# Attention values of branch A issued as unbroken trains of matmuls, ahead of other waiting matmuls

## The chip, the cores and the metric

The kernel runs on one core of a Trainium2 chip. The metric is the device time of one execution in microseconds (us). Each time in this document is from the runs of the kernel or from a hardware profile of one execution. The engines are named as in the profile: PE is TensorE's matmul, PEld its weight load, DVE is VectorE, ACT is ScalarE, POOL is GpSimd and SP is SyncE, which issues all transfers. L915 means line 915 of the kernel.

## The reference

One encoder layer is applied to two groups of requests (a prompt and a sample, 1024 tokens each, width 1024) with the same weights. The input is normalised and modulated, one combined projection gives everything that the two attention branches need, and the two results are gated, projected, merged and projected again:

```python
h = rms_norm(x, norm_g) * (1.0 + scale) + shift
proj = einsum('bsd,de->bse', h, w_in)
qa, ka, va, za, qb, kb, vb, zb, ga, gb = split(proj, ...)
# branch A: 8 query heads, 2 key/value heads, head width 64, two-dimensional rotary positions
oa = gqa_attention(rope(rms_norm(qa)), rope(rms_norm(ka)), va) * silu(za)
# branch B: 4 heads, the difference of two softmax maps, values 128 wide
ob = headnorm(diff_attention(qb, kb, vb, lam)) * silu(zb)
merged = sigmoid(ga) * (oa @ w_proj_a) + sigmoid(gb) * (ob @ w_proj_b)
y = x + gate * (merged @ w_out)
```

Branch A is plain attention: softmax over all 1024 keys, then probabilities times values:

```python
s = einsum('bqgrd,bkgd->bgrqk', q, k) / sqrt(64)
p = softmax(s)
o = einsum('bgrqk,bkgd->bqgrd', p, v)
```

Everything is in fp32.

## The kernel before, in words

The two groups are worked one after the other. For each, a start computes the normalised input (for group 0 from the beginning, for group 1 behind group 0's output projection), then come the projections, branch A's attention, branch B's attention, the gates, the merge and the output projection. Most matmuls take operands split into a high and a low part, in three products; the value matmuls of both branches take plain fp32.

Branch A's attention is cut into 32 units a group: a unit is two query heads that share a key/value head, for a tile of 128 queries. For each of its two heads `scores` runs four 512-wide matmuls (L846, L847) into one of two score banks, then DVE takes the maximum (L848), ACT scales it (L849) and takes the exponential (L850). `flip` transposes the 128x1024 probabilities in 32x32 blocks on DVE (L891) and issues four transfers from SP (L896) that put the blocks into the tile `pT` (the tiles named q in the profile), half of it for each head. The value step `a_values` (L908 on) then takes for each of eight chunks of 128 keys and each of the two heads one matmul: weights are the 128x64 values of the chunk, the moving side is 128x128 of the transposed probabilities, and the output is one half of the partitions of the bank `acc`. The loop runs over chunks, and within a chunk over the heads e = 0, 1, so that head 0 stands in the left 64 columns of the array and head 1 in the right 64. So there are 16 value matmuls a unit, 512 a group. ACT copies the bank out (L922), and every second unit a transfer stores it (L925). There is a single bank for this.

What sets the order is a scheduler. The Python code writes the attention as a generator and weaves it with other generators (projections of later heads, the z, g gates: L608, L819, L668) by weights: `ATT_W` scales how fast a phase's attention advances against its filling, `IN_A` gives the filling a head start. A phase is one piece of this: 0 and 1 are branch A's two halves, 2 and later are branch B's heads. The recorded instructions then go to a scheduler with a model of the machine, which sends each engine the instruction that it takes for the best next one among those that could run, by a priority that follows the order of recording. `tc.high_priority(offset=n)` moves what is recorded inside it n places ahead; all of the attention's steps stand in one of `AHEAD = 100`. Each engine then runs its instructions strictly in the order that the scheduler has set.

```python
            with tc.high_priority(offset=AHEAD):
                ...
                    next(vals[n], None)
```

Of the kernel before, what the change touches and what calls it, by code (L numbers as in the profile page):

```python
# [23 lines left out]
NCH = D // P  # L24
# [16 lines left out]
Z_HEAD = (7, 6)  # L41
Z_HEAD_A = (-0.3, -0.32)
ATT_W = (
    (0.825, 1.067, 1.07, 1.093, 1.03, 1.769),
    (0.938, 1.664, 1.177, 1.271, 0.764, 1.144),
)
IN_A = (
    (0.3, -0.07, 0.7, 0.05, 0.25, 0.15),
    (0.1, -0.05, 0.33, 0.3, -0.03, 0.55),
)  # L50
Z_A = (
# [21 lines left out]
AHEAD = 100  # L73
PV_LAG = 2
A_WAIT = 1
A_CUTS = ()

WHOLE = (True, True)

# [30 lines left out]
def kernel(ctx: ExitStack, tc: tile.TileContext, t: dict):  # L110
    nc = tc.nc
# [18 lines left out]
    def nm(s):  # L130
        uid[0] += 1
        return f"{s}_{uid[0]}"
# [40 lines left out]
    def mtile(tag, shape, dt=F32, bufs=None):  # L173
        return mpool.tile(shape, dt, tag=tag, name=nm(tag), bufs=bufs)
# [733 lines left out]
    def a_values(u):  # L908
        acc = ps_a.tile([P, 512], F32, tag="a", name=nm("a"))[:, :P]
        pT = u["pT"].bitcast(F32).rearrange("p (i t c b) -> p t c i b", i=4, t=2, c=8)  # L910
        for _ in range(A_WAIT):
            yield 1
        for k in range(NCH):
            for e in range(2):
                nc.tensor.matmul(acc[e * 64 : e * 64 + 64], u["v"](k), pT[:, e, k], start=(k == 0), stop=(k == 7))  # L915
            if k in A_CUTS:
                yield 1
        t = u["qt"] % 2
        if t == 0:
            turned["o"] = mtile("oo", [P, 256])  # L920
        o = turned["o"]
        nc.scalar.activation(o[:, t * P : (t + 1) * P], acc, AF.Copy)  # L922
        pr = u["pr"]
        if t:
            dma(u["od"][pr // 2][:, (pr % 2) * 256 : (pr % 2 + 1) * 256], o)  # L925
        yield 1
# [408 lines left out]
```

## Time and profile before

| | |
|---|---|
| median of 3 runs | 2003.58 us (2002.83 to 2007.69) |
| the profiled execution | 2004.5 us, its span 2002.7 us |
| granted TensorE clock, mean over the span | 0.993 |
| PE busy | 1951.8 us, 97% of the span |
| DVE, ACT, POOL busy | 61%, 43%, 20% of the span |
| value matmuls of branch A (L915) | busy 195.4 us, 2048 records, mean 281 ns of one |

The span is the time from the first to the last instruction; the device time is a little longer. "Busy" is the time in which at least one instruction of the row runs. Matmuls are pipelined: a 128x512 one lasts 0.39 us in the profile, but in a row they start 0.227 us apart, so steps are read from starts. An fp32 value matmul is two passes, and the profile has a record for each. The first value matmul of group 0 starts at 137.9 us and branch A of that group lasts until about 592; that of group 1 lasts from 1151 to 1484.

### The profile page before, as it was taken

The numbers are of one execution on the slowest core, as the hardware profiler recorded it, in microseconds if no ns is written. First come the engines' busy times: TensorE is split into PE (matmuls) and PEld (weight loads), VectorE is DVE, ScalarE is ACT, GpSimd is POOL, SyncE is SP. The second block draws the span as 40 slices with busy tenths as digits, with TensorE's granted clock in tenths as the row PEclk, the third lists the DMA queues.
The fourth block names the chain that finished last, engine by engine and source line by source line (L and its number), as shares of the span: only waits on it lengthen the run. The fifth ranks groups of instructions, "written<-read, shape, count | busy, mean of one in ns | idle before, by whom it ended". The sixth has DMA issues, their size and how long they took to land.

```text
span 2002.7 us, 32130 instructions
## 1 busy us (share of the span) xinstructions
PE 1951.8 (97%) x11430; PEld 1606.1 (80%) x11430; DVE 1213.9 (61%) x1824; ACT 853.1 (43%) x1839; POOL 400.7 (20%) x766
## 2 busy tenths in 40 slices
PE   6899999999999999999999999999999999999999
PEld 4778777777788888877889977788888899877787
DVE  4765565333457857786575665665536776877731
ACT  3544444233455645442423444554435554643210
POOL 0433200001232524100023312100044332400000
PEclk9999999999999999999999999999999999999999
DMA  9134566453435533788562274676633443478622
GB/s 320 39 90 134 132 187 167 127 136 102 111 109 160 143 104 81 209 260 277 194 198 71 86 186 127 174 190 163 165 98 97 124 110 99 126 222 281 213 100 74
DMA packets 277630, 299.55 MB, mean 150 GB/s; under 512 B 37664, under 2 KB 228320, under 8 KB 277472
## 3 DMA queue, kind: packets, MB, share of 16 engines
q1 hardware_dynamic: 277472, 297.51, 52.4%
q8 instruction: 92, 1.51, 0.3%
q14 instruction: 66, 0.54, 0.1%
HBM read 137.91 MB, written 42.04 MB: 90 GB/s over the span
## 4 chain that ended last, share of the span: by engine, by line
PE 84%; DMA 6%; DVE 5%; ACT 2%; issue 1%; POOL 1%; SPq 1%; DVEq 0%; ACTq 0%; POOLq 0%
PE f L819 24%; PE f L608 19%; PE a L915 9%; PE s L846 6%; PE f L1119 5%; PE s L847 5%; PE a L944 4%; PE s L1119 3%; PE f L1088 3%; PE s L1088 2%; PE s L106 1%; DMA row<-zd 1%; PE f L668 1%; DVE m L848 1%; DVE p L890 1%
## 5 line engine op out<-in xcount | busy, mean ns | idle before, releaser
L819 PE MATMUL f<-u,w 128*128 128x512 f32 x2184 | 577.2, 398 | 2.2 <-ACT ev L801 1.5
L608 PE MATMUL f<-w,u 128*128 128x256 f32 x3264 | 478.5, 288 | 4.2 <-DVE u L106 1.7
L819 PEld LDWEIGHTS f<-u,w 128*128 128x128 f32 x2184 | 397.5, 188 | 92.5 <-issue 14.7
L608 PEld LDWEIGHTS f<-w,u 128*128 128x128 f32 x3264 | 434.2, 191 | 37.4 <-issue 14.6
L848 DVE TENSOR_REDUCE m<-s 128x1 f32<-128x1024 f32 x256 | 310.7, 1218 | 227.3 <-PE s L847 225.3
L891 DVE STREAM_TRANSPOSE p<-p 128x1024 f32<-128x1024 f32 x192 | 238.4, 1242 | 94.6 <-ACT p L850 81.1
L847 PE MATMUL s<-u,sw 128*128 128x512 f32 x512 | 206.3, 404 | 0.0
L915 PE MATMUL a<-q,u 128*64 128x128 f32 x2048 | 195.4, 281 | 0.0
L915 PEld LDWEIGHTS a<-q,u 128*64 128x64 f32 x2048 | 129.8, 136 | 66.7 <-issue 49.4
L205 DVE TENSOR_TENSOR w<-st,w 128x512 fp32r<-128x512 f32 x188 | 125.4, 699 | 68.6 <-ACT w L204 66.7
L204 ACT ACTIVATE w<-st 128x512 fp32r<-128x512 f32 x188 | 108.7, 625 | 129.9 <-DMA st<-in_w_in_dram 52.7
L850 ACT ACTIVATE p<-s,m,rsB 128x1024 f32<-128x1024 f32 x128 | 154.2, 1205 | 5.2 <-DVE p L890 1.6
L850 ACT ACTIVATE p<-s,m,rsA 128x1024 f32<-128x1024 f32 x128 | 154.2, 1205 | 4.0 <-PE a L915 0.2
L1088 PE MATMUL f<-u,w 128*128 128x512 f32 x576 | 141.4, 395 | 5.1 <-ACT u L1060 3.0
L764 POOL TENSOR_TENSOR row<-row,gB 128x96 f32<-128x96 f32 x64 | 30.2, 472 | 549.0 <-ACT row L629 548.9
L1088 PEld LDWEIGHTS f<-u,w 128*128 128x128 f32 x576 | 108.2, 189 | 29.7 <-ACT u L1060 3.4
L944 PE MATMUL a<-q,u 128*128 128x256 f32 x512 | 126.0, 381 | 3.0 <-DMA q<-p 1.6
L671 DVE TENSOR_TENSOR u<-f,u 64x256 fp32r<-64x256 f32 (+1 forms) x208 | 84.1, 406 | 61.3 <-ACT u L670 55.8
L846 PE MATMUL s<-u 128*128 128x512 f32 x256 | 110.8, 433 | 4.2 <-ACT p L850 4.1
L847 PEld LDWEIGHTS s<-u,sw 128*128 128x128 f32 x512 | 97.0, 190 | 20.0 <-issue 5.0
L1119 PE MATMUL f<-u,w 128*128 128x512 f32 x480 | 111.2, 389 | 0.0
L628 ACT ACTIVATE row<-f 128x256 f32<-128x256 f32 (+1 forms) x104 | 38.5, 370 | 167.0 <-PE f L608 162.7
(191 smaller groups left out, 2216.9 us busy)
## 6 DMA issues: line engine op xcount, KB each, us to landing
q<-p SPq DMA_DIRECT2D x768, 128.0 KB, 2.8
st<-in_w_in_dram SPq DMA_DIRECT2D x128, 256.0 KB, 3.4
zd<-ev SPq DMA_DIRECT2D x96, 256.0 KB, 2.7
sw<-u SPq DMA_DIRECT2D x256, 64.0 KB, 2.1
p<-zd SPq DMA_DIRECT2D x64, 256.0 KB, 4.3
u<-in_w_ada_dram SPq DMA_DIRECT2D x16, 512.0 KB, 8.9
od<-oo SPq DMA_DIRECT2D x64, 128.0 KB, 2.5
st<-in_w_in_dram SPq DMA_DIRECT2D x64, 128.0 KB, 2.8
```

The costliest lines, as they stand in the source:

```text
L205: nc.vector.tensor_tensor(out=wl, in0=st, in1=wh.bitcast(F32), op=ALU.subtract)
L608: nc.tensor.matmul(ps, lt[c][:, sl], w[c][:, wi, :], start=(k == 0), stop=(k == 23))
L819: nc.tensor.matmul(ps, w[c][:, wi, e * P : (e + 1) * P], rt[c], start=(k == 0), stop=(k == 23),)
L846: nc.tensor.matmul(s[:, sl], q, k[:, sl], start=True, stop=False)
L847: nc.tensor.matmul(s[:, sl], sw, k[:, sl], start=False, stop=True)
L848: nc.vector.tensor_reduce(out=m, in_=s, axis=AX.X, op=ALU.max, negate=True)
L850: nc.scalar.activation(pt.rearrange("p (j c a) -> p j c a", j=4, c=8), s.rearrange("p (c a j) -> p j c a", c=8, j=4), AF.Exp, scale=rs, bi ...
L891: nc.vector.transpose(pt, pt)
L915: nc.tensor.matmul(acc[e * 64 : e * 64 + 64], u["v"](k), pT[:, e, k], start=(k == 0), stop=(k == 7))
L944: nc.tensor.matmul(acc, u["v"][:, k], pT[:, k], start=(k == 0), stop=(k == 7))
L1088: nc.tensor.matmul(ps, w[:, c, wi, d * P : (d + 1) * P], o[:, oi, :], start=(k == 0), stop=(k == 11))
L1119: nc.tensor.matmul(ps, w[c][:, wi, e * P : (e + 1) * P], m[:, mi, :], start=(k == 0), stop=(k == 23))
```

## The change

Three things. In `a_values` the 16 matmuls of a unit are recorded inside a second priority block, 200 places ahead (`TRAIN`), and the heads are taken in the order 1, 0. The possible pause between chunks (`A_CUTS`, empty before) is gone. Two numbers that weave the phases of group 0's branch B are others: the attention's weight in phase 3 and the filling's head start in phase 2.

```diff
 ATT_W = (
-    (0.825, 1.067, 1.07, 1.093, 1.03, 1.769),
+    (0.825, 1.067, 1.07, 1.192, 1.03, 1.769),
     (0.938, 1.664, 1.177, 1.271, 0.764, 1.144),
 )
 IN_A = (
-    (0.3, -0.07, 0.7, 0.05, 0.25, 0.15),
+    (0.3, -0.07, 0.65, 0.05, 0.25, 0.15),
     (0.1, -0.05, 0.33, 0.3, -0.03, 0.55),
 )
...
-A_CUTS = ()
+TRAIN = 200
...
         for _ in range(A_WAIT):
             yield 1
-        for k in range(NCH):
-            for e in range(2):
-                nc.tensor.matmul(acc[e * 64 : e * 64 + 64], u["v"](k), pT[:, e, k], start=(k == 0), stop=(k == 7))
-            if k in A_CUTS:
-                yield 1
+        with tc.high_priority(offset=TRAIN):
+            for k in range(NCH):
+                for e in (1, 0):
+                    nc.tensor.matmul(
+                        acc[e * 64 : e * 64 + 64], u["v"](k), pT[:, e, k], start=(k == 0), stop=(k == 7)
+                    )
```

What this does to the order on PE shows best in a unit from the middle of group 0's branch A (its accumulator is a_4202). Before, near the end of that unit; L819 and L608 are projections that fill:

```order
L608 MATMUL f_3978<-w_3955,u_433 128x256
L819 MATMUL f_4052<-u_632,w_3713 128x512
L915 MATMUL a_4202<-q_4027,u_728 64x128
L819 MATMUL f_4052<-u_631,w_3713 128x512
L915 MATMUL a_4202<-q_4027,u_728 64x128
L608 MATMUL f_3978<-w_3955,u_433 128x256
L608 MATMUL f_3978<-w_3955,u_434 128x256
```

The unit's 16 value matmuls stand one by one in 16 places. The same unit on PE after the change:

```order
L819 MATMUL f_4052<-u_649,w_3713 128x512
L819 MATMUL f_4052<-u_648,w_3713 128x512
L608 MATMUL f_4096<-w_3955,u_275 128x256
L916 MATMUL a_4202<-q_4027,u_728 64x128 x16
L608 MATMUL f_4096<-w_3955,u_275 128x256
L608 MATMUL f_4096<-w_3955,u_276 128x256
```

All 16 follow each other, at a place where one fill tile has just ended and the next has begun. Not every unit is whole: the last unit of each group's branch A is still cut, here that of group 0 on PE (accumulator a_5519; L668 are transposes of projected rows):

```order
L819 MATMUL f_5090<-u_433,w_5073 128x512
L916 MATMUL a_5519<-q_5003,u_728 64x128 x3
L668 MATMUL f_5109<-ident,row_4908 128x128 x2
L916 MATMUL a_5519<-q_5003,u_728 64x128
L608 MATMUL f_5139<-w_5116,u_275 128x256
L916 MATMUL a_5519<-q_5003,u_728 64x128
L608 MATMUL f_5139<-w_5116,u_275 128x256
```

Over the whole program the value matmuls of branch A stood in 272 unbroken runs on PE, 182 of them of one matmul, and stand now in 72, of which 62 have 16. The other engines have the same instructions in another order.

## Prediction

> **What bounds the kernel now.** I read the page's busy table first, then the busy time by stage, then TensorE's own timeline.
>
> ```profile
> span 2002.7 us, 32130 instructions
> PE 1951.8 (97%) x11430; PEld 1606.1 (80%) x11430; DVE 1213.9 (61%) x1824; ACT 853.1 (43%) x1839; POOL 400.7 (20%) x766
> ```
>
> TensorE (PE) is busy for 97% of the span and no other engine for more than 61%. Cut into stages (the start, branch A of group 0, branch B of group 0 with its ending, then the same two for group 1):
>
> ```profile
> core 0: us, PE busy (x) PEld busy (x) DVE busy (x) ACT busy (x) POOL busy (x), PEclk, DMA share, GB/s
> 0.00:138.00 138.00, 110.59 (x655) 90.64 (x656) 83.11 (x197) 61.19 (x138) 37.96 (x67) 0.93 0.51 155
> 138.00:592.00 454.00, 454.00 (x2763) 342.34 (x2763) 223.30 (x274) 183.64 (x398) 65.77 (x125) 1.00 0.50 133
> 592.00:1151.00 559.00, 545.64 (x3016) 468.04 (x3017) 389.24 (x648) 245.80 (x534) 144.72 (x266) 1.00 0.54 161
> 1151.00:1484.00 333.00, 332.97 (x2325) 267.83 (x2324) 191.86 (x216) 151.93 (x327) 40.45 (x75) 1.00 0.62 161
> 1484.00:2002.70 518.70, 508.64 (x2679) 437.25 (x2675) 326.36 (x493) 210.49 (x444) 111.78 (x236) 1.00 0.48 143
> ```
>
> In the two branch A stages, 454 and 333 us long, PE has no idle time at all and a granted clock of 1.00. What shortens PE's work there shortens the stage, until another engine or a transfer ends last. The same view for the value line (L915) alone:
>
> ```profile
> core 0: us, PE busy (x) PEld busy (x), PEclk, DMA share, GB/s
> 138.00:592.00 454.00, 113.28 (x1024) 67.89 (x1024) 1.00 0.50 133
> 1151.00:1484.00 333.00, 81.79 (x1024) 61.75 (x1024) 1.00 0.62 161
> ```
>
> The program has 512 value matmuls in each stage, and the trace 1024 records: an fp32 matmul is recorded as two passes. The same work takes 113 us in one stage and 82 in the other. The order tells why: I call an unbroken run of value matmuls on PE a *stay*. Before, group 0 has 188 stays and group 1 has 84; 182 of the 272 hold one matmul.
>
> **The price of a stay** comes from starts, since the ends of matmuls are modelled. Here a whole unit stands as one stay of 16 (32 records):
>
> ```profile
> 1338.98 0.87 PE L608 MATMUL f<-w,u 128*128 128x256 f32 x6
> 1339.78 1.97 PE L915 MATMUL a<-q,u 128*64 128x128 f32 x32
> 1341.68 0.50 PE L846 MATMUL s<-u,u 128*128 128x512 f32 x1
> 1342.02 0.40 PE L847 MATMUL s<-u,sw 128*128 128x512 f32 x1
> ```
>
> Six L608 matmuls last 0.87 with a last one of 0.27, so they step by 0.12, and a seventh would have started at 1339.70: 0.08 are lost on the way in. The stay holds PE for 1.90, until 1341.68. The score matmul behind it then steps by 0.34 instead of 0.23: 0.11 lost on the way out. Together 2.09 us. Of these the 16 matmuls in 8 pairs, the two heads on the two column halves at once, take 8 x 2 x 0.109 = 1.74 (the pass step seen inside such a stay), which leaves 0.35 for the stay itself. Now lone ones, between 256-wide and between 512-wide matmuls:
>
> ```profile
> 454.10 0.39 PE L608 MATMUL f<-w,u 128*128 128x256 f32 x1
> 454.41 0.43 PE L915 MATMUL a<-q,u 128*64 128x128 f32 x2
> 454.77 0.39 PE L608 MATMUL f<-w,u 128*128 128x256 f32 x1
> 455.09 0.43 PE L915 MATMUL a<-q,u 128*64 128x128 f32 x2
> ...
> 1320.55 0.39 PE L847 MATMUL s<-u,sw 128*128 128x512 f32 x1
> 1320.87 0.43 PE L915 MATMUL a<-q,u 128*64 128x128 f32 x2
> 1321.23 3.70 PE L819 MATMUL f<-u,w 128*128 128x512 f32 x15
> ```
>
> The first kind repeats every 0.68, of which the L608 alone would take 0.12: 0.56. In the second the next matmul was due at 1320.78 and starts at 1321.23, and the 15 behind it last 3.70 instead of 14 x 0.227 + 0.39 = 3.57: 0.58. A lone matmul takes a whole pair's time, 0.218, since its column half has no partner; 0.56 to 0.58 less 0.218 leaves 0.34 to 0.36. So: **0.35 us for each stay, plus 0.218 for each pair or lone matmul in it.**
>
> **The change part by part.** *The trains.* Counted in the instruction order, with a stay of an odd number rounded up to pairs:
>
> - group 0: 188 stays and 334 pair times become 38 and 259: 150 x 0.35 + 75 x 0.218 = 52.5 + 16.4 = 68.9 us;
> - group 1: 84 and 293 become 34 and 256: 50 x 0.35 + 37 x 0.218 = 17.5 + 8.1 = 25.6 us.
>
> Sum 94.4 us. Nothing is added: the matmuls and their weight loads are the same 1024. Check of the counts: 334 and 293 pair times with 0.226 of each stay (of 1.97, the part that the busy rows see, less 1.744) give 115 and 83; the two L915 rows have 113.3 and 81.8. A second check, adding up all steps into, inside and out of the stays over the whole trace, gives 137 + 93 = 230 us for branch A's values, where 0.35 and 0.218 give 232. I keep 94.
>
> A rule of the Trainium skill speaks against the pairing part. "TensorE: Matmul & The Clock Gate", section "Part 3: Packing small matmuls", says that a weight load overlaps matmuls in flight only when its row group differs; both heads here use all rows, so by it a pair would gain nothing over two lone matmuls, the gain would be the stays alone, 70 us, and the time 1940. The trace does not agree: two loads (132 to 137 ns each in the rows below) and two passes fit into 109 ns.
>
> *The order of the heads and the place.* All 16 matmuls now stand behind the later head's transposed probabilities, and ahead of other work.
>
> ```profile
> L915 PEld LDWEIGHTS a<-q,u x2048: 132/137/137, 137.9 to 1483.8; 128*64 128x64 f32 x187
> L915 PE MATMUL a<-q,u x2048: 272/273/324, 137.9 to 1484.0; 128*64 128x128 f32 x187
> ...
>   DMA q<-p: 0.7, 2
> ```
>
> Before, PE waited 0.7 us in all for these transfers. One head's way there:
>
> ```profile
> 1330.71 1.23 DVE L848 TENSOR_REDUCE m<-s 128x1 f32<-128x1024 f32 x1 [0.67 <-PE s L847]
> ...
> 1333.53 1.20 ACT L850 ACTIVATE p<-s,m,rsA 128x1024 f32<-128x1024 f32 x1
> ...
> 1334.86 1.25 DVE L891 STREAM_TRANSPOSE p<-p 128x1024 f32<-128x1024 f32 x1 [0.65 <-ACT p L850]
> ...
> 1337.80 3.08 SPq L896 DMA_DIRECT2D q<-p  x4
> ...
> q<-p SPq DMA_DIRECT2D x768, 128.0 KB, 2.8
> ...
> 1345.41 0.43 PE L915 MATMUL a<-q,u 128*64 128x128 f32 x2
> ```
>
> Maximum at 1330.7, exponential, transpose until 1336.1, four transfers issued from 1337.8 (SP was issuing weights until then); the last is issued at about 1340.3 and lands 2.8 later, at 1343.1. The first value matmul comes 2.3 us after. Over the 64 units the first matmul of the later head starts 0.6 to 18 us after its landing, median 3.6. A unit's stretch of PE loses 68.9/32 = 2.15 us in group 0 and 25.6/32 = 0.8 in group 1, which comes out of this margin. Four units of group 0 and one of group 1 have less; they lack 2.3 us together. That is the lower end but for zero; the upper end is a train that stands just at its landing, where half of the 64 come early by the scatter of such chains (9 to 14 us from maximum to landing, so about 1 us each): some 30 us. I take 6, near the lower end, since in the new order the trains stand 10 to 16 us of PE steps behind their unit's last score matmul, median 13.5, no nearer than before.
>
> Everything else issued for a unit (copy L922, store L925, transposes, score matmuls) is the same and only stands in another order. Score banks: the two alternate, and the new order leaves at least 4.8 us of PE steps between a bank's last matmul and its next use, where maximum and exponential need 1.2 + 0.3 + 1.2; so nothing there. The other engines get denser: group 0's stage would be 385 us, DVE 223/385 = 58%, ACT 48%. That is what group 1's stage already has (192/333 = 58%, 46%) with PE never idle. This cover is the reason to cost the rest at nothing.
>
> *The pieces set anew* act on two phases of group 0's branch B. In 592 to 1151 PE is idle for 13.4 us. The bounds are 13 us of gain, if all of it went, and as much of loss; I take 0.
>
> **Sum.** 2002.7 - 94.4 + 6 = 1914.3 us of span. The profiled execution took 2004.5, 1.8 more than its span, and the median of the runs is 2003.58, 0.9 below that execution. 1914.3 + 1.8 = 1916 us.
>
> **Rivals.**
>
> *The trains wait.* If the new place is at the landing rather than after it, PE gives back 0.5 us a train, 32 us: 1942. For it: the train goes ahead of all that waits, so in the scheduler's eyes it stands at the first moment. Against: 0.7 us of such waits before, margins of 3.6.
>
> *Branch B gives it back.* The whole order behind the change is made anew. If branch B's two stages, 1078 us with 23 us idle, went to twice that idle time: 1916 + 23 = 1939. For it: their order differs too; against: their work and priorities are nearly the same.
>
> *Slower: the queue of transfers decides.* SP issues every transfer in order. The pieces of group 1's branch A:
>
> ```profile
> L896 SPq DMA_DIRECT2D q<-p x251: 542/602/1994, 1150.6 to 1455.7; - x126
> ```
>
> These are 251 of 389 issues in that stage; at 0.594 us on average the 389 fill 231 of the 333 us, and 75% of the 308 that would be left. If the trains' pieces queue there behind weights and gates, each train blocks PE with all score matmuls behind it, and so the next unit's chain too. From 94/64 = 1.5 us a train the gain is gone; at 3 us it is 1916 + 64 x 3 = 2108. Against: SP still has 102 us free in that stage, and 25.6 go. The skill's page "TensorE: Matmul & The Clock Gate", in "What overlaps and what doesn't", has matmuls run in strict order without reordering, so a waiting train does hold all behind it; the trace has no such wait to test that on.
>
> *It does not do what it says.* If the stay's price hung on the neighbours and not on the switch, it would not go: 70 of 94 us stay, 1986. The 0.35 found beside 120 and 227 ns neighbours alike speaks against it.
>
> **How the numbers follow.** Forecast 0.64, trains wait 0.17, branch B 0.10, price that stays 0.04, slower 0.05. Faster 0.93 from the first four less a little for mixtures that end near nothing; within 0.3% (6 us, about what a measurement here can tell from no change) 0.02; slower 0.05. The forecast's own range is 1903 (no wait, and 7 us of branch B's idle time gone) to 1932 (16 us of waits or idle more). To 1950 it takes in the two milder rivals, and leaves out the last two and a few mishaps. So 1902 to 1950.
>
> **What would show it.** Right: value matmuls in 72 stays, their busy time near 65 and 64 us in the two branch A stages, these about 387 and 309 us long with PE still without idle time, the other stages as they are. PE idle before the value line on DMA q<-p of tens of us is the first rival; PE busy falling short in the branch B stages the second; SP's waits gone and landings late the third. Stays gone, with the branch A stages no shorter and PE full, would make the price wrong, and the prediction with it.

## The result, and the profile after

The changed kernel takes 1910.63 us (median of 4 runs, 1909.6 to 1912.61), the kernel before 2004.93 us (median of 4 runs). The ratio is 0.953 with a 95% interval of 0.9514 to 0.9547: 94 us faster. The profiled execution took 1911.05 us, its span 1909.3.

The page's busy table of the changed kernel:

```profile
span 1909.3 us, 32080 instructions
PE 1860.2 (97%) x11430; PEld 1589.6 (83%) x11430; DVE 1212.0 (63%) x1824; ACT 851.0 (45%) x1839; POOL 398.9 (21%) x766
```

The same 11430 matmul records keep PE busy for 92 us less; DVE and ACT are busy for as long as before. By stage, cut at the first and the last value matmul of each group:

```profile
core 0: us, PE busy (x) PEld busy (x) DVE busy (x) ACT busy (x) POOL busy (x), PEclk, DMA share, GB/s
152.00:513.00 361.00, 361.00 (x2615) 307.20 (x2615) 203.66 (x245) 167.62 (x365) 53.97 (x104) 1.00 0.61 161
513.00:1091.00 578.00, 565.35 (x3122) 486.03 (x3121) 400.41 (x664) 256.19 (x558) 151.13 (x280) 0.99 0.54 159
1091.00:1393.00 302.00, 302.00 (x2294) 257.01 (x2294) 185.99 (x211) 148.36 (x321) 38.90 (x72) 1.00 0.66 173
1393.00:1909.30 516.30, 505.87 (x2674) 435.49 (x2672) 326.38 (x492) 209.85 (x443) 112.01 (x236) 1.00 0.49 143
```

Both branch A stages are shorter and PE still has no idle time in them. The same cut for the value line alone, which is now L916:

```profile
core 0: us, PE busy (x) PEld busy (x), PEclk, DMA share, GB/s
152.00:513.00 361.00, 64.90 (x1024) 55.73 (x1024) 1.00 0.61 161
1091.00:1393.00 302.00, 63.42 (x1024) 55.21 (x1024) 1.00 0.66 173
```

113 and 82 us have become 65 and 63 for the same 1024 records. PE's timeline at one train of the changed kernel:

```profile
1364.09 0.40 PE L608 MATMUL f<-w,u 128*128 128x256 f32 x2
1364.42 1.97 PE L916 MATMUL a<-q,u 128*64 128x128 f32 x32
1366.32 1.81 PE L608 MATMUL f<-w,u 128*128 128x256 f32 x13
```

It is the form of stay that already stood in the kernel before at 1339.78, 1.90 us from its start to the next matmul's. No row of the changed kernel names a wait of the value line for its transfers (q<-p).

### The profile page after: what moved, and what is told of

Its sections match the earlier page's. It is cut to its first block, busy times and chain, and to the rows that moved or that the text cites. A ratio compares the mean times of both kernels' runs of the same rounds, so it can differ in the third digit from the quotient of the medians.

```text
span 1909.3 us, 32080 instructions
## 1 busy us (share of the span) xinstructions
PE 1860.2 (97%) x11430; PEld 1589.6 (83%) x11430; DVE 1212.0 (63%) x1824; ACT 851.0 (45%) x1839; POOL 398.9 (21%) x766
## 4 chain that ended last, share of the span: by engine, by line
PE 50%; DMA 3%; DVE 2%; ACT 1%; issue 1%; POOL 0%; SPq 0%; DVEq 0%; ACTq 0%; POOLq 0%
PE f L819 12%; PE f L608 10%; PE f L1120 6%; PE f L1089 4%; PE s L1120 3%; PE a L916 3%; PE s L846 3%; PE s L847 3%; PE a L945 2%; PE s L1089 2%; DMA row<-zd 1%; DMA tab<-rB 1%; PE f L668 0%; DMA st<-in_w_in_dram 0%; DMA q<-p 0%
## 5 line engine op out<-in xcount | busy, mean ns | idle before, releaser
L819 PE MATMUL f<-u,w 128*128 128x512 f32 x2184 | 559.2, 394 | 3.0 <-ACT ev L801 1.9
L819 PEld LDWEIGHTS f<-u,w 128*128 128x128 f32 x2184 | 399.7, 188 | 84.0 <-ACT ev L801 2.4
L608 PE MATMUL f<-w,u 128*128 128x256 f32 x3264 | 458.9, 287 | 3.1 <-DVE u L106 1.7
L608 PEld LDWEIGHTS f<-w,u 128*128 128x128 f32 x3264 | 430.3, 192 | 24.9 <-issue 3.6
L1089 PE MATMUL f<-u,w 128*128 128x512 f32 x576 | 141.7, 396 | 5.4 <-ACT u L1061 3.2
L916 PE MATMUL a<-q,u 128*64 128x128 f32 x2048 | 128.3, 276 | 0.0
L916 PEld LDWEIGHTS a<-q,u 128*64 128x64 f32 x2048 | 110.9, 137 | 19.6 <-issue 11.6
L1120 PE MATMUL f<-u,w 128*128 128x512 f32 x480 | 111.2, 389 | 0.0
L945 PEld LDWEIGHTS a<-q,u 128*128 128x128 f32 x512 | 93.9, 190 | 17.2 <-issue 3.4
```

Source lines behind the costliest of these rows:

```text
L608: nc.tensor.matmul(ps, lt[c][:, sl], w[c][:, wi, :], start=(k == 0), stop=(k == 23))
L819: nc.tensor.matmul(ps, w[c][:, wi, e * P : (e + 1) * P], rt[c], start=(k == 0), stop=(k == 23),)
L945: nc.tensor.matmul(acc, u["v"][:, k], pT[:, k], start=(k == 0), stop=(k == 7))
L1089: nc.tensor.matmul(ps, w[:, c, wi, d * P : (d + 1) * P], o[:, oi, :], start=(k == 0), stop=(k == 11))
L1120: nc.tensor.matmul(ps, w[c][:, wi, e * P : (e + 1) * P], m[:, mi, :], start=(k == 0), stop=(k == 23))
```

## The experiments

In all of them I add up, over the trace, what the stays take of PE ("values"): the time from a stay's first start to the next matmul's start, and what the matmul before it and the one behind it take beyond their usual step (0.12 us for 256 columns, 0.227 for 512). What is left of the span is "the rest". "By the price" is 0.35 us for each stay and 0.218 us for each pair time.

| | stays | pair times | by the price, us | values, us | span, us | rest, us |
|---|---|---|---|---|---|---|
| before | 272 | 627 | 232 | 230.0 | 2002.7 | 1772.7 |
| changed | 72 | 515 | 138 | 137.6 | 1909.3 | 1771.7 |
| two numbers alone | 272 | 627 | 232 | 230.0 | 2003.0 | 1773.0 |
| trains, old numbers | 72 | 515 | 138 | 137.6 | 1908.4 | 1770.8 |
| trains, heads 0, 1 | 134 | 577 | 173 | 173.7 | 1947.3 | 1773.6 |
| heads 1, 0 alone | 237 | 595 | 213 | 211.3 | 1985.1 | 1773.8 |

The theory is that the price of the stays is the whole gain. The rivals are that the two new numbers carry part of it, or that the place ahead of other work does.

**The two numbers.** Alone, in the kernel before:

```diff
-    (0.825, 1.067, 1.07, 1.093, 1.03, 1.769),
+    (0.825, 1.067, 1.07, 1.192, 1.03, 1.769),
-    (0.3, -0.07, 0.7, 0.05, 0.25, 0.15),
+    (0.3, -0.07, 0.65, 0.05, 0.25, 0.15),
```

> The kernel before with the two new numbers of the weaving alone; the value matmuls stand in 272 stays as before. Theory (the gain is the price of the stays, 0.35 us each and 0.218 us for each pair or lone matmul): no change, 2005 us within 6. Rival (the new numbers carry part of the gain, by less idle time in branch B of group 0): faster by up to the 13 us that PE is idle there.

Measured 2004.86 us against 2004.77 before; ratio 1.0008 (0.9998 to 1.0018). And taken back in the changed kernel (the same lines the other way):

> The changed kernel with the two old numbers of the weaving; 72 stays as in the changed kernel. Theory: 1911 us within 6, the whole gain without the numbers. Rival (the numbers carry part of it): slower than 1911 by 5 us or more.

Measured 1912.17 us, ratio 0.9544 (0.9527 to 0.9561), which the changed kernel's interval overlaps. The numbers do nothing that can be measured.

**The order of the heads, with and without the priority block.** In the changed kernel the old order:

```diff
-                for e in (1, 0):
+                for e in (0, 1):
```

> The changed kernel with the heads in the old order 0, 1 inside the priority block. In the instruction order the first matmul of head 0 now leaves alone and the other 15 follow as a train: 134 stays and 577 pair times instead of 72 and 515. Theory: 62 x 0.35 + 62 x 0.218 = 35 us more than the changed kernel, 1946 us. Rival (the place ahead of other work makes the gain, and not the number of stays): 1911 us.

Measured 1947.32 us, ratio 0.9712 (0.9689 to 0.9736). PE's timeline shows what the late head does:

```profile
309.44 0.61 PE L819 MATMUL f<-u,w 128*128 128x512 f32 x2
309.99 0.43 PE L916 MATMUL a<-q,u 128*64 128x128 f32 x2
310.35 0.74 PE L608 MATMUL f<-w,u 128*128 128x256 f32 x4
311.02 1.96 PE L916 MATMUL a<-q,u 128*64 128x128 f32 x30
312.92 0.50 PE L846 MATMUL s<-u,u 128*128 128x512 f32 x1
```

One matmul of head 0 goes as soon as it can, PE changes back to L608, and the other 15 come later. The train then lasts as long as one of 16, since its last matmul has no partner. So inside the block this order is worth 36 us of values (173.7 less 137.6), and the block with the old order 56 (230.0 less 173.7). In the kernel before, the new order without the priority block:

```diff
-            for e in range(2):
+            for e in (1, 0):
```

> The kernel before with the heads in the order 1, 0 and no priority block: 237 stays and 595 pair times instead of 272 and 627. Theory: 35 x 0.35 + 32 x 0.218 = 19 us less than before, 1986 us. Rival (the place ahead of other work makes the gain): 2005 us, since nothing is moved ahead.

Measured 1986.53 us, ratio 0.9913 (0.9894 to 0.9932). With nothing put ahead the time follows the stays, and both kernels fall within 2 us of what the price gives. The rest in the table is the same within 3 us in all six kernels, with and without the block. So the price of the stays is shown, and the block gains through the number of stays alone.

**Do pairs share their time?** In the changed kernel the loops swapped:

```diff
-            for k in range(NCH):
-                for e in (1, 0):
+            for e in (1, 0):
+                for k in range(NCH):
```

> The changed kernel with the two loops swapped: in each train first the 8 matmuls of head 1, then the 8 of head 0, so that no two neighbours stand on different column halves. 72 stays as in the changed kernel. Theory (a pair on both halves takes the time of one): 1024 lone matmuls instead of 515 pair times, 509 x 0.218 = 111 us more, 2022 us. Rival, from the Trainium skill, page TensorE: Matmul & The Clock Gate, section Part 3: Packing small matmuls (a weight load hides behind matmuls in flight only when its row group differs): pairing gains nothing here, 1911 us.

One run (the runs of any one kernel above lie within 10 us of each other): 1999.01 us, 88 more than the changed kernel; the values take 224.1 us, 86.5 more, and the rest is 1773.1. A stay on PE's timeline:

```profile
305.21 3.33 PE L916 MATMUL a<-q,u 128*64 128x128 f32 x32
308.46 0.73 PE L846 MATMUL s<-u,u 128*128 128x512 f32 x2
```

PE is held for 3.25 us instead of 1.90; 64 x 1.35 = 86. So pairing is real: neighbours of different heads share time, neighbours of the same head don't. Two heads differ in the column half and in the part of the bank that they add to; this run does not part the two. The rule that the rival has from the Trainium skill, that a load hides only beside another row group, does not fit these column halves. My 111 us were too many: two runs of 8 should take 16 x 0.109 = 1.74 longer, and 0.39 of it are missing. The steps of such a stay say why: 109 ns each, but for a longer first one, until the 13th pass, then 6, 104, 56, 53, 56, 53, 57, then 109 again. If two passes on one half start at least 109 apart, as they do everywhere else in these stays, three passes of the second head run beside the last three of the first; that is inferred, since a record does not say which head it is.

**How near are the trains to waiting?** In the changed kernel the first matmul of a train starts 0.3 to 8.7 us after the last landing of its pieces, median 2.4 in group 0 and 1.9 in group 1 (before, for the later head: 4.8 and 3.3). To see how much of SyncE's queue this margin needs, more transfers were put between those of `flip`:

```diff
             dma(dst[:, i, t], pt[i * 32 : i * 32 + 32])
+            if "j" in u and i < 2:
+                dma(dpool.tile([32, 1024], F32, name=nm("xd")), pt[i * 32 : i * 32 + 32])
```

> The changed kernel with two more transfers for each head of branch A, 256 in all: two of the four pieces of the transposed probabilities are also written to scratch in DRAM that nobody reads. This adds about 256 x 0.55 = 141 us of SyncE's issue time and no other work: by stage 246 + 70 = 316 of 388 us and 231 + 70 = 301 of 316 us. Theory (PE sets the end as long as the issues fit into the stage): 1911 to 1920 us. Rival (the trains already stand close to their landings, margin 0.3 to 2.4 us, so that any delay in SyncE's queue becomes PE idle): 64 trains by about 1 us, 1975 us.

One run: 1997.11 us, 86 more. My theory fell here. PE's waits over the whole span, what the exponential waited for in the first branch A stage, and the two branch A stages:

```profile
PE a L918 <- DMA q<-p: 29.4, 16, 4.9
PE s L846 <- ACT p L850: 28.7, 12, 8.5
```

```profile
ACT p L850 <- DMA q<-p: 12.1, 4, 5.6
```

```profile
156.00:557.00 401.00, 372.17 (x2601) 314.07 (x2596) 201.16 (x242) 165.65 (x359) 52.72 (x102) 0.96 0.69 184
1137.00:1479.00 342.00, 310.64 (x2272) 262.17 (x2269) 186.33 (x209) 148.32 (x318) 36.99 (x70) 0.97 0.75 200
```

PE has 60 us of idle time in the stages where it had none: trains wait for their pieces, and score matmuls for a bank whose exponential came late. In the first stage the exponential itself waited 12.1 us for transfers that had to free its tile; in the changed kernel it has no such wait. The mean granted clock falls to 0.96 and 0.97; as an estimate, 401 x 0.04 + 342 x 0.03 = 26 us. With the 60 that is the 86.

SyncE's own rows show how full its queue is:

```profile
1204.98 0.60 SPq L896 DMA_DIRECT2D q<-p  x1
1205.62 0.59 SPq L898 DMA_DIRECT2D xd<-p  x1
1206.26 0.59 SPq L896 DMA_DIRECT2D q<-p  x1
1206.89 0.59 SPq L898 DMA_DIRECT2D xd<-p  x1
```

An issue lasts 0.59 us, and the next one starts about 0.05 later. The issues alone fill 299 of 401 and 296 of 342 us; with these short gaps it is 327 and 324 us, 82% and 95% (255 of 361 and 245 of 302 us, 71% and 81%, in the changed kernel). So in group 1 the issues no longer fit into the 302 us that the stage had, and my condition was not met: I had reckoned 0.55 us for each added issue and no gaps. In group 0 they still fit, and that stage grew by 40 us too: there a delay in the queue is enough. With all four pieces (the same without `and i < 2`):

> The same with all four pieces written to scratch as well, 512 more transfers, about 280 us of SyncE's issue time: 246 + 140 = 386 of 388 us and 231 + 140 = 371 of 316 us. Theory: the second branch A stage becomes bound by the issues, 371 - 316 = 55 us more, 1966 us, with PE idle there for transfers. If PE alone set the end: 1911 us.

One run: 2106.95 us, far over both figures. With the short gaps SyncE is occupied for 397 of 430 and 396 of 423 us, 92% and 94%, and the stages grow by 69 and 122 us. These 397 and 396 us are more than the 361 and 302 us that the stages had, so the issues now bound both stages and not the second alone; the mechanism of my theory was there, its price for an issue was too low. To tell the issue time from the bytes, the 256 extra transfers were made small:

```diff
-                dma(dpool.tile([32, 1024], F32, name=nm("xd")), pt[i * 32 : i * 32 + 32])
+                dma(dpool.tile([32, 8], F32, name=nm("xd")), pt[i * 32 : i * 32 + 32, :8])
```

> As the run with two more transfers for each head, but each of the 256 carries 1 KB instead of 128 KB, at nearly the same place of the queue. Theory (SyncE's issue time, about 0.58 us each whatever the size, makes the trains late): about the same as with the large ones, 1985 to 2000 us, if the issue of a small one lasts as long. Rival (the bytes crowd the DMA engines): 1911 to 1920 us.

One run: 2001.03 us. The issue of a small one takes as long (median 587 ns in both), and it does as much harm. It is the time in SyncE's queue, not the bytes.

**Fewer stays still.** The block at 800 places makes the last units whole as well:

```diff
-TRAIN = 200
+TRAIN = 800
```

> The changed kernel with the priority block at 800 places instead of 200: the last units of both groups are whole trains too, 64 stays and 512 pair times instead of 72 and 515. Theory: 8 x 0.35 + 3 x 0.218 = 3.5 us less than the changed kernel, 1907 us. Rival (the last units' trains, put further ahead, wait for their transfers or hold up the first work of the next phase): 1911 us or more.

Measured 1918.74 us, ratio 0.9575 (0.9562 to 0.9589): slower than the changed kernel, though the values take 135.0 us, 2.6 less. The rest is 1782.0, 10 more. Most of it went in branch B of group 0; PE's timeline at one place and the granted clock (the third number from the end) in two windows:

```profile
629.13 0.48 PE L847 MATMUL s<-u,sw 128*128 128x512 f32 x1
632.44 1.01 PE L549 MATMUL f<-two,row 128*128 128x2 f32 x4 [2.83 <-DVE row L546]
633.32 0.79 PE L846 MATMUL s<-u 128*128 128x512 f32 x1
633.91 0.63 PE L847 MATMUL s<-u,sw 128*128 128x512 f32 x1
634.34 0.63 PE L846 MATMUL s<-u 128*128 128x512 f32 x1
```

```profile
630.00:636.00 6.00, 3.56 (x16) 2.29 (x20) 5.79 (x12) 4.08 (x8) 2.98 (x6) 0.64 0.74 196
636.00:642.00 6.00, 6.00 (x42) 4.72 (x35) 5.46 (x8) 2.83 (x7) 0.34 (x1) 0.79 0.26 69
```

A wait of 2.83 us for a DVE copy, then a granted clock of 0.64 and 0.79: 6.8 us at half clock, in which score matmuls step by 0.43 and more instead of 0.23. Behind the start there are four such stretches of 24 us in all here, and three of 10 us in the changed kernel. So a wait can be paid for once more after it. The trains themselves got cheaper. Group 0's branch B, where three of the four stretches are, stands in another order on PE. The fourth is in group 1's, where PE's order for the last 2597 records is the same in both kernels and takes 507 us instead of 505; over the kernels of the table the same order of this branch B takes 516 to 521, so that this part is scatter.

Two units in one stay, the later one first, both halves of one bank, one copy, and also 800 places ahead. The value steps of branch A are recorded sooner for it (`behind`, 0.95 instead of 1.4). Cut to the main lines:

```diff
-        acc = ps_a.tile([P, 512], F32, tag="a", name=nm("a"))[:, :P]
+        us = turned["first"], u
+        acc = ps_a.tile([P, 512], F32, tag="a", name=nm("a"))[:, : 2 * P]
...
+            for t in (1, 0):
+                for k in range(NCH):
+                    for e in (1, 0):
...
-            steps += [(n + BEHIND + i / nv, ph, n, i, False) for i in range(nv)]
+            behind = 0.95 if ph < 2 else BEHIND
+            steps += [(n + behind + i / nv, ph, n, i, False) for i in range(nv)]
```

> The changed kernel with the value matmuls of two units in one stay of 32, both halves of one bank, the later unit first, 800 places ahead; one copy of the bank for both. 32 stays and 512 pair times instead of 72 and 515. Theory: 40 x 0.35 + 3 x 0.218 = 15 us less, 1896 us. Rival (the earlier unit's transposed tile is held longer, there are only two such tiles, so the next unit's transfers wait and the trains come late): 32 stays by 1 to 2 us of PE idle, 1928 to 1960 us.

Measured 1912.00 us, ratio 0.9535 (0.9518 to 0.9552): no gain. The rival isn't it, since the value line waits 0.6 us in all. PE's timeline and the accounts show the gain and where it went; here is a stay, from the last run below:

```profile
314.29 0.39 PE L819 MATMUL f<-u,w 128*128 128x512 f32 x1
314.61 3.71 PE L920 MATMUL a<-q,u 128*64 128x128 f32 x64
318.26 0.50 PE L846 MATMUL s<-u,u 128*128 128x512 f32 x1
```

32 matmuls hold PE for 3.65 us; with 0.10 lost on the way in and 0.10 on the way out it is 3.85, where two stays of 16 take 2 x 2.09 = 4.18: the price of one stay less. The values need 124.2 us, 13.4 less than in the changed kernel, but the rest is 1786.5, 15 more. Two other orders of branch B with the same stays were tried, first with the two old numbers of the weaving, then with a third pair (1.0 and 0.55):

> The kernel with stays of two units, with the two old numbers of the weaving. Branch A's instructions are in the same stays (32 of 32 matmuls), only branch B of group 0 is ordered otherwise. Theory (branch A's gain of 13 us is there in every order, and what branch B loses by waits and the half clock behind them is a matter of each order): values of branch A cost 124 us again, and all else anything between 1771 and 1787 us, so 1897 to 1913 us. Rival (stays of two units cost branch B something of their own): 1911 us or more again.

> The same with a third pair of numbers (weight 1.0 instead of 1.192, head start 0.55 instead of 0.65). Theory: 124 us for the values of branch A, 1897 to 1913 us in all, not the same as the other two. Rival: 1911 us or more in all three.

Measured 1906.09 us (0.9507; 0.9493 to 0.9521) and 1903.18 us (0.9492; 0.9474 to 0.951). The values take 125.0 and 125.8 us, and the rest 1778.3 and 1774.9. Branch A's gain is there each time, and with the same stays the rest varies by 12 us with the order of branch B. But in all four kernels with 800 places the rest is 1775 us or more, and in the six of the table it is 1774 or less. So a cost of some 3 us that these kernels bring of themselves is not ruled out. The last is the fastest kernel here, 7 us below the changed one; its interval ends just below the changed kernel's.

## Why the prediction was right, point by point

- *The price of a stay and of a pair time.* Shown. The values went from 230.0 to 137.6 us where 232 and 138 were worked out, a gain of 92.4 against 94.4, and the kernels with 134, 237, 64 and 32 stays lie within 3 us of it.
- *Trains wait, 6 us.* The sign of the margin was right, its size not: it fell by 2.4 and 1.4 us in the two groups (2.15 and 0.8 were worked out), but no train waited. The 6 us did not come, and neither did the first rival. That is what puts the measured 1910.6 below 1916: the profiled span is 5 us under the forecast one, 6 of them from here and 1 from the rest, less the 2 by which the values' gain fell short.
- *The other engines, at no cost.* Right: DVE has 204 of 361 and 186 of 302 us, and PE no idle time there.
- *The pieces, 0.* Shown, in both directions.
- *Length of the stages.* Wrong: 387 and 309 us were named, cut from 138 us on. From the first to the last value matmul they are 361 and 302 us. The new order also moves work out of these stages: group 0's has 1591 other matmul records where it had 1739, and the first value matmul comes at 152 us instead of 138. The sum did not rest on this.
- *Branch B gives it back.* Not here: the rest is 1771.7 against 1772.7. But the mechanism is real, as the four kernels with 800 places show with 1775 to 1787.
- *The queue of transfers decides.* Not here, but its size was misread. I summed the issues alone and called the remaining 102 us of the old second stage free. With the 0.05 us between two issues SyncE was occupied for 250 of those 333 us, and in the changed kernel's 302 for 245: 81%, not 75%. So some 57 us were left. 256 issues more cost 86 us, where the queue became 95% full and also where it stayed at 82%: there the margin of the trains, about 2 us, and the waits for tiles that the transfers free were what gave way.

## What to carry to other kernels

Where matmuls on parts of the array's columns stand among full ones, count the changes to and fro: each pair of changes cost 0.35 us here, and a matmul without its partner on the other half costs the partner's time too. To keep them together, put what becomes ready last first, so that the group starts only when all of it can run, and then put it ahead; the first of these was worth 36 us of the 94 inside the priority block and 18 without it. Before densifying a stage further, look at the margin between the last landing and its first use, and reckon the issuing queue from one issue's start to the next's: 256 transfers more, with which the queue was occupied for 82% and 95% of the two stages, took back 86 of the 94 us.

## What the runs showed of the hardware that was not expected

- PE seems not to wait for one column half's run to end before it begins the other's: in the run with the heads one after the other, three passes of the second head run beside the last three of the first. That is inferred from the steps (6, 104, 56, 53, 56, 53, 57 ns among steps of 109), since a record does not say which head it is.
- The issue of a transfer takes SyncE 0.59 us, and the next one starts 0.05 us later, for 1 KB and for 128 KB alike.
- Waits of PE of 2.0 to 3.2 us behind the start are each followed by 3.4 or 6.8 us at half clock in the changed kernel and in the one with 800 places. That loses 1.7 or 3.4 us each, so that such a wait cost 1.5 to 2.2 times what its row says. The length of the wait alone does not decide it: in two of the kernels with stays of two units, waits of 1.6, 1.9 and 1.98 us had such a stretch behind them, and in the kernel before one of 3.0 us had none. Here is that one, on PE's timeline and with the granted clock of 1.00 around it:

```profile
933.59 0.50 PE L1088 MATMUL f<-u,w 128*128 128x512 f32 x1 [3.00 <-ACT u L1060]
```

```profile
930.00:934.00 4.00, 1.00 (x5) 0.53 (x4) 1.82 (x4) 0.63 (x1) 0.00 (x0) 1.00 0.92 290
934.00:940.00 6.00, 6.00 (x27) 4.54 (x25) 4.64 (x9) 2.46 (x4) 0.00 (x0) 1.00 0.90 252
```
